# Gate columns of an mLSTM branch taken from a value projection instead of from products of their own

## The chip, the cores and the metric

The kernel runs on one core of one Trainium2 chip. The metric is the device time of one execution in microseconds. The chip was run on the kernel before three times: 1974.41, 1974.73 and 1976.49 us, median 1974.73 us.

## What is computed

The reference is a two-layer backbone over 512 latent tokens and 256 context tokens of width 1024, all in float32. Each layer normalises and modulates its input (h), projects it once, runs three mixers side by side (A: differential attention, B: a bidirectional chunkwise mLSTM, C: neighbourhood attention), gates each, merges them and adds the result. The change concerns the 16 gate columns of mixer B, `bg`: two directions, input and forget gate, four heads.

```
aq, ak, av, az, bq, bk, bv, bo, bz, bg, cq, ck, cv, cz, gm = split_proj(h @ w_in)
...
gates = g.reshape(B, T, 2, 2, ML_HEADS).astype(jnp.float32) + gate_b.astype(jnp.float32)
log_i = gates[:, :, :, 0]
log_f = jax.nn.log_sigmoid(gates[:, :, :, 1])
```

From `log_i` and `log_f` mixer B forms running sums and running maxima along the tokens, forwards and backwards, and from these the weights of its attention-like products. Mixer C's values, `cv`, are 512 other columns of the same projection.

## The kernel before

The activations h lie transposed, eight tiles of 128 channels by 768 tokens (512 latent, then 256 context), each as a pair: the value rounded to the matmul's type and the remainder. A weight is split into such a pair too. A product of both is three matmuls (`P3`, line 32). Weights arrive in halves of a unit, 128 x 512 numbers, in the ring `wr`; ScalarE (ACT) casts the rounded part into the ring `wh`, and GpSimd (POOL) or VectorE (DVE) forms the remainder (`Stream.step`, `Stream.lower`). `wh` has four buffers.

Each layer goes through mixer C, mixer A, mixer B, the merge and the output projection. A projection with channels on the partitions (`proj`: keys `ck`, queries `cq`, gates `cz`) takes weights as the stationary operand and 512 latent or 256 context tokens as the moving one. A value projection (`proj_v`: `cv`, `av`, `bv`) takes 128 tokens of h as the stationary operand and 256 weight columns as the moving one. It makes six token tiles of 24 matmuls, each into one buffer of the PSUM ring `pj`, which has two. The code behind a tile (`fin`) copies it out on ACT and DVE and then releases the buffer.

The gate columns are made while the first value projection of mixer C (`cv`, 0) runs. Its caller hands it a function, `hook`. Called ahead of token tile 4 and once more behind tile 5, it is `gate_mm`: 16 matmuls over the 512 latent tokens, then 16 over the 256 context tokens, with 32 stationary columns (the 16 gate weights and their remainders, `wg`). The result, 32 rows by 768 tokens, is copied to a tile `t`. Four matmuls in full float32 with a matrix of ones and zeros (`zsrc`) spread it over 112 rows, one for each direction, head and chunk of 64 tokens, once for the forget gate and once for the input gate. What follows in `fin` of `branch_b_gates` is a chain on [112, 768] rows, mostly on DVE: log-sigmoid, two running sums, a running maximum, reordering, two stores, twelve transposes and 24 small copies into `bcol`. Mixer B waits for its end much later.

The order of the instructions on each engine is made while the program is built. `Sched` keeps a clock for each engine, from a table of costs, and lists of unfinished work (urgent, calm and other chains). Whenever the main line, which issues the projections in a fixed order, reaches a slot, chains that are due by these clocks issue their next step. So a change of a few instructions moves the places at which others are put. On the chip each engine runs its instructions in the order so made.

## Time and profile before

| | us |
|---|---|
| median of three runs | 1974.73 |
| lowest and highest | 1974.41, 1976.49 |
| the profiled execution | 1975.63 |
| its span, first to last instruction | 1973.9 |
| TensorE (PE) busy | 1865.8 |
| VectorE (DVE) busy | 1363.2 |
| ScalarE (ACT) busy | 862.1 |
| GpSimd (POOL) busy | 617.3 |

The profile is one execution. Its views are: a page with busy times; a timeline, in which instructions of a kind are merged, with the start, the length, the operation, what it writes and reads, the count, and the idle time of the engine ahead of it with what ended that; and windows, which give each engine's busy time, the granted clock of TensorE as a share of 2.4 GHz, and the transfers. A name such as `pj<-h,wh` means that `pj` is written from `h` and `wh`. All of a helper's instructions carry the helper's line, so the names tell them apart. Lengths of matmuls overlap; how far apart they are is read from their starts.

### The profile page before, as it was taken

The page shows a single profiled execution, that of the slowest core. Times are in us where ns is not written, and L with a number is a line of the kernel's source. Part 1 is how long each engine was busy: PE and PEld are TensorE (multiplying, and loading weights), DVE is VectorE, ACT ScalarE, POOL GpSimd, SP SyncE. Part 2 cuts the span into 40 slices and gives each one's busy share as a digit, 9 for nine tenths or more (in the row PEclk, how much of TensorE's full clock was granted, in tenths as well). Part 3 has the DMA queues.
Part 4 walks back from the last instruction along what each step waited for, and adds up shares of the span by engine and source line. Part 5 has one row for each costly group of instructions (what it writes and reads, how often), then busy time and mean ns, then how long its engine had stood idle before and what let it go on. Part 6 is the DMA issues. An engine that isn't in the chain of part 4 may idle for free.

```text
span 1973.9 us, 31993 instructions
## 1 busy us (share of the span) xinstructions
PE 1865.8 (95%) x11420; PEld 1636.1 (83%) x11420; DVE 1363.2 (69%) x3165; ACT 862.1 (44%) x1972; POOL 617.3 (31%) x498
## 2 busy tenths in 40 slices
PE   5989999999999999999999898999999999999997
PEld 2879998988889888888887777898979787888886
DVE  6587775888787877687835768676887777743336
ACT  4345544555544553222223444555555444433343
POOL 1242322121222222333334533424222323334454
PEclk9989999999999999999999999999999999999998
DMA  8233323222211122566645423333231212335554
GB/s 316 72 96 102 96 79 97 61 82 65 68 51 51 44 83 76 182 227 200 214 152 169 147 78 111 119 94 109 69 105 54 65 50 69 97 109 186 168 167 124
DMA packets 137247, 222.26 MB, mean 113 GB/s; under 512 B 15984, under 2 KB 47776, under 8 KB 137088
## 3 DMA queue, kind: packets, MB, share of 16 engines
q1 hardware_dynamic: 137088, 220.22, 35.6%
q8 instruction: 91, 1.49, 0.3%
q14 instruction: 68, 0.56, 0.1%
HBM read 177.36 MB, written 28.11 MB: 104 GB/s over the span
## 4 chain that ended last, share of the span: by engine, by line
PE 47%; issue 21%; DVE 17%; POOL 9%; ACT 3%; DMA 2%; SPq 0%; POOLq 0%; DVEq 0%; ACTq 0%
PE pj L379 34%; POOL wh L344 8%; PE gp L379 7%; PE gp L383 3%; DVE p L344 3%; PE sc L379 3%; DVE qk L344 2%; DVE pt L344 2%; DVE t L344 1%; DMA cb<-in_wmodr_dram 1%; DVE v L344 1%; DVE sc L344 1%; ACT wh L344 1%; DVE h L344 1%; ACT p L344 1%
## 5 line engine op out<-in xcount | busy, mean ns | idle before, releaser
L379 PE MATMUL pj<-h,wh 128*128 128x512 f32 (+1 forms) x5664 | 1124.4, 351 | 20.1 <-DVE gz L344 9.9
L379 PEld LDWEIGHTS pj<-h,wh 128*128 128x128 f32 x5664 | 897.3, 191 | 144.0 <-DVE gz L344 10.3
L344 POOL TENSOR_TENSOR wh<-wr,wh 128x512 fp32r<-128x512 f32 x409 | 558.9, 1372 | 1269.4 <-ACT wh L344 1250.8
L344 ACT CAST wh<-wr 128x512 fp32r<-128x512 f32 x416 | 256.9, 620 | 395.5 <-PE pj L379 193.4
L379 PE MATMUL pj<-wh,h 128*128 128x256 f32 x1728 | 239.3, 289 | 4.1 <-DVE h L344 2.5
L379 PEld LDWEIGHTS pj<-wh,h 128*128 128x128 f32 x1728 | 219.7, 193 | 7.1 <-DVE h L344 3.7
L344 DVE TENSOR_TENSOR pt<-gp,pt 128x512 fp32r<-128x512 f32 (+1 forms) x224 | 123.6, 572 | 80.2 <-ACT pt L344 79.2
L344 ACT CAST pt<-gp 128x512 fp32r<-128x512 f32 (+1 forms) x224 | 105.1, 497 | 155.6 <-PE gp L383 155.1
L379 PE MATMUL pj<-v,wh 128*128 128x512 f32 (+1 forms) x576 | 161.6, 357 | 6.5 <-DVE t L344 6.2
L383 PE MATMUL gp<-ident,p 128*128 128x128 f32 x720 | 110.3, 278 | 23.4 <-DVE p L344 15.5
L379 PEld LDWEIGHTS pj<-v,wh 128*128 128x128 f32 x576 | 103.5, 189 | 23.9 <-DVE t L344 7.9
L379 PE MATMUL gp<-pt,v 128*128 128x256 f32 x864 | 120.2, 287 | 0.0
L383 PEld LDWEIGHTS gp<-ident,p 128*128 128x128 f32 x720 | 84.0, 142 | 40.4 <-issue 18.1
L379 PEld LDWEIGHTS gp<-pt,v 128*128 128x128 f32 x864 | 113.0, 195 | 2.0
L344 ACT ACTIVATE t<-pj 128x512 f32<-128x512 f32 (+1 forms) x118 | 63.4, 538 | 99.7 <-PE pj L379 93.5
L379 PE MATMUL pj<-qk,wh 128*128 128x512 f32 (+1 forms) x288 | 102.2, 355 | 0.0
L344 DVE TENSOR_REDUCE mna<-sc 128x1 f32<-128x768 f32 (+1 forms) x80 | 67.8, 847 | 38.5 <-PE sc L379 38.3
L344 DVE SCALAR_TENSOR_TENSOR t<-t,pj 128x512 f32<-128x512 f32 x66 | 38.8, 594 | 73.2 <-PE pj L379 71.2
L344 ACT ACTIVATE p<-sc,mna 128x768 f32<-128x768 f32 (+1 forms) x80 | 65.5, 819 | 53.7 <-DVE mna L344 53.5
L379 PE MATMUL sc<-qk 128*128 128x512 f32 (+1 forms) x360 | 82.0, 336 | 5.0 <-ACT p L344 4.9
L344 DVE CUSTOM_DVE_ANT_0 sc<-cb,prm 128x512 f32<-128x512 f32 x56 | 60.0, 1072 | 25.4 <-DMA cb<-in_wmodr_dram 24.1
L344 DVE TENSOR_TENSOR qk<-t,qk 64x768 fp32r<-64x768 f32 (+1 forms) x64 | 64.0, 1000 | 14.2 <-ACT qk L344 11.8
(157 smaller groups left out, 2208.8 us busy)
## 6 DMA issues: line engine op xcount, KB each, us to landing
wr<-in_wu_dram SPq DMA_DIRECT2D x304, 256.0 KB, 2.9
cb<-in_wmodr_dram SPq DMA_DIRECT2D x64, 256.0 KB, 3.4
wr<-in_wout_dram SPq DMA_DIRECT2D x64, 256.0 KB, 2.8
wr<-in_wbr_dram SPq DMA_DIRECT2D x48, 256.0 KB, 2.9
q<-qk SPq DMA_DIRECT2D x160, 64.0 KB, 2.4
cb<-vd SPq DMA_DIRECT2D x32, 256.0 KB, 3.2
qk<-in_xT_dram SPq DMA_DIRECT2D x16, 384.0 KB, 5.0
pd<-t SPq DMA_DIRECT2D x16, 384.0 KB, 3.9
```

Of the source, the lines that this page charges most:

```text
L344: return f(*args, **kw)
L379: PE.matmul(o, l, r, start=start, stop=stop)
L383: PE.transpose(o, i, idn)
```

## The change

The 16 gate columns are appended to the weights of the first value projection of mixer C, which then has 272 columns (a new input `wcv`, the value and gate columns side by side). Each token tile gets its gate columns as columns 256 to 271 of its PSUM buffer. `fin` of `proj_v` then calls the hook, which is now `spread`: two copies on DVE write the tile's gate columns, repeated twelve times over the chunks, to one of two tiles `t`, six blocks of 112 columns with tokens on the partitions. When all six tiles are spread, twelve transposes bring them to 112 rows by tokens, where the four selecting products stood before. The gate weights `wg`, their load, cast and remainder, `gate_mm` and the selection matrix go. The rings `wr` and `wh` get buffers for 544 columns in place of 512. The two tiles `t` are held from the first token tile to the last transpose.

```
@@ _units
+            cols = base + np.arange(256)
+            u.append((key + (hf,), np.concatenate([cols, BG + np.arange(16)]) if key == ("cv", 0) else cols, hf))
@@ setup
-            SY.dma_start(out=rv, in_=a["wbg"][l])
-            V.tensor_copy(wg[l][:, :, 0:16], rv)
-            V.tensor_tensor(wg[l][:, :, 16:32], rv, wg[l][:, :, 0:16].bitcast(F32), ALU.subtract)
@@ Stream.step
+                n = int(stream[i].shape[-1]) // 2
+                t = ring("wr", [2 * wide])[:, :n]
+                SY.dma_start(out=t, in_=stream[i][:, n * hf:n * hf + n])
...
+                w = ring("wh", [2, 2 * wide], F32R)[:, :, :int(src.shape[-1])]
@@ proj_v
+            nw = wide if hook else 256
-                if j == 4 and hook:
-                    S_.until(lambda: ready.n == DEPTH)
-                    hook(0)
...
+                        mm(ps[:, :nw], h[k][:, hb, 128 * j:128 * j + 128], w[:, wa, c0:c0 + nw],
...
+                    if hook:
+                        yield from hook(j, ps[:, 256:wide])
                     rel("pj")
...
-            if hook:
-                hook(1)
@@ branch_b_gates
-            def gate_mm(s):
...
-                        mm(ps[:32, :n], wg[l][:, k, :], h[k][:, b, o:o + n], k == 0 and b == 0, k == 7 and b == 1)
...
+            def spread(j, src):
+                if j == 0:
+                    for i in range(2):
+                        yield from acq("t")
+                        gx[i] = ring("t", [T])
+                        pad = gx[i][:, 0:6 * R].rearrange("p (j x) -> p j x", x=R)[:, :, 48:64]
+                        GP.memset(pad, 0.0)
+                while gx[j // 3] is None:
+                    yield
+                for gi in range(2):
+                    o0 = R * (2 * (j % 3) + gi)
+                    to = gx[j // 3][:, o0:o0 + R]
+                    to = bass.AP(to.tensor, to.offset, [list(to.ap[0]), [64, 2], [12, 4], [1, 12]])
+                    V.tensor_copy(to, src.rearrange("p (d g h) -> p d g h", d=2, g=2)[:, :, gi]
+                                  .unsqueeze(3).to_broadcast([128, 2, 4, 12]))
+                hit(gflag)
...
-                yield from wait(gflag, 2, "P")
+                yield from wait(ready, DEPTH)
+                yield from wait(gflag, NT, "P")
...
-                        mm(p[:R, :n], zsrc[0:32, 48 + R * gi:48 + R * gi + R], gr[0][:32, o:o + n], True, True)
+                        for b in range(n // 128):
+                            j = o // 128 + b
+                            o0 = R * (2 * (j % 3) + gi)
+                            tr(p[:R, 128 * b:128 * b + 128], gx[j // 3][:, o0:o0 + R], ident)
...
-                rel("t")
+                rel("t"), rel("t")
```

The change moves instructions that it doesn't name, since the scheduler's clocks differ. The order differs from the first value projection of layer 0 to the first part of mixer A there, and in layer 1 from the first value projection to the first part of mixer A; elsewhere it is the same. Three places follow, before and after.

TensorE in layer 0, from the first value projection (`pj<-wh,h`) to the first keys (`pj<-h,wh`), before:

```order
L379 MATMUL pj<-wh,h 128x256 x96
L379 MATMUL pj<-h,wg_173 32x512 x16
L379 MATMUL pj<-wh,h 128x256 x48
L379 MATMUL pj<-h,wg_173 32x256 x16
L379 MATMUL pj<-h,wh 128x512 x3
L379 MATMUL gp<-t,zsrc 112x512
L379 MATMUL pj<-h,wh 128x512 x9
L379 MATMUL gp<-t,zsrc 112x256
L379 MATMUL pj<-h,wh 128x512 x6
L379 MATMUL gp<-t,zsrc 112x512
```

and after:

```order
L381 MATMUL pj<-wh,h 128x272 x144
L381 MATMUL pj<-h,wh 128x512 x12
L385 MATMUL gp<-ident,t 112x128 x4
L381 MATMUL pj<-h,wh 128x512 x9
L385 MATMUL gp<-ident,t 112x128 x2
L381 MATMUL pj<-h,wh 128x512 x3
L381 MATMUL pj<-h,wh 128x256 x6
L385 MATMUL gp<-ident,t 112x128 x4
L381 MATMUL pj<-h,wh 128x256 x18
L385 MATMUL gp<-ident,t 112x128 x2
```

The gate products are gone, and the transposes (`gp<-ident,t`) stand in four groups, the first behind twelve key products.

VectorE in layer 0, in the chain of the gates: `v` and `pt` of 112 rows are the chain (the scans are listed as `SCALAR_TENSOR_TENSOR pt<-pt,t` and `v<-v,pt`), `gz<-gz,pj` empties a PSUM buffer of the gate projection `cz`, `qk<-t,qk` belongs to mixer C's keys and queries. Before:

```order
L344 TENSOR_TENSOR v<-v 112x768 x2
L344 SCALAR_TENSOR_TENSOR pt<-pt,v 112x768
L344 SCALAR_TENSOR_TENSOR pt<-pt,t 112x768
L344 TENSOR_TENSOR qk<-t,qk 64x768 x2
L344 SCALAR_TENSOR_TENSOR pt<-pt,t 112x768
L344 TENSOR_TENSOR v<-pt 112x768
L344 TENSOR_TENSOR v<-v,pt 112x767
L344 SCALAR_TENSOR_TENSOR gz<-gz,pj 128x512
L344 SCALAR_TENSOR_TENSOR v<-v,pt 112x768
L344 TENSOR_TENSOR wh<-wr,wh 128x512
L344 TENSOR_TENSOR v<-pt,v 112x768
L344 SCALAR_TENSOR_TENSOR gz<-gz,pj 128x256
```

and after:

```order
L345 TENSOR_TENSOR v<-v 112x768 x2
L345 TENSOR_TENSOR qk<-t,qk 64x768
L345 SCALAR_TENSOR_TENSOR pt<-pt,v 112x768
L345 TENSOR_TENSOR qk<-t,qk 64x768
L345 SCALAR_TENSOR_TENSOR pt<-pt,t 112x768 x2
L345 SCALAR_TENSOR_TENSOR gz<-gz,pj 128x512
L345 TENSOR_TENSOR v<-pt 112x768
L345 TENSOR_TENSOR wh<-wr,wh 128x512
L345 TENSOR_TENSOR v<-v,pt 112x767
L345 SCALAR_TENSOR_TENSOR gz<-gz,pj 128x256
```

The first `gz<-gz,pj` stood behind `v<-pt` and `v<-v,pt` and now stands ahead of both. In layer 1 it stood behind both scans and `v<-pt` and now stands between the two scans.

VectorE in layer 1, where the context part of h (`qk<-qk,gsc,gp` and `h<-qk,modc,h` of 256 tokens) is made during the first value projection, whose tiles leave by `v<-pj,v`. Before:

```order
L344 TENSOR_TENSOR v<-pj,v 128x2x128
L344 SCALAR_TENSOR_TENSOR qk<-qk,gsc_186,gp 128x256 x5
L344 SCALAR_TENSOR_TENSOR h<-qk,modc_184,h 128x256 x3
L344 TENSOR_TENSOR v<-pj,v 128x2x128
L344 SCALAR_TENSOR_TENSOR h<-qk,modc_184,h 128x256 x2
L344 SCALAR_TENSOR_TENSOR qk<-qk,gsc_186,gp 128x256 x3
L344 SCALAR_TENSOR_TENSOR h<-qk,modc_184,h 128x256
L344 COPY t<-pj 32x512
L344 SCALAR_TENSOR_TENSOR h<-qk,modc_184,h 128x256 x2
L344 TENSOR_TENSOR v<-pj,v 128x2x128
```

and after:

```order
L345 TENSOR_TENSOR v<-pj,v 128x2x128
L345 COPY t<-pj 128x2x48 x2
L345 SCALAR_TENSOR_TENSOR qk<-qk,gsc_184,gp 128x256 x5
L345 SCALAR_TENSOR_TENSOR h<-qk,modc_182,h 128x256 x3
L345 TENSOR_TENSOR v<-pj,v 128x2x128
L345 COPY t<-pj 128x2x48 x2
L345 SCALAR_TENSOR_TENSOR h<-qk,modc_182,h 128x256 x2
L345 SCALAR_TENSOR_TENSOR qk<-qk,gsc_184,gp 128x256 x3
L345 SCALAR_TENSOR_TENSOR h<-qk,modc_182,h 128x256 x3
L345 TENSOR_TENSOR v<-pj,v 128x2x128
L345 COPY t<-pj 128x2x48 x2
```

Two copies (`t<-pj`, 2 x 48) stand behind each token tile, two pairs of them within this part of h; the copy of 512 gate columns is gone.

## Rows read from the trace of the kernel before

**Rows 1.** The page, part 1: busy us, share of the span, instructions.

```profile
PE 1865.8 (95%) x11420; PEld 1636.1 (83%) x11420; DVE 1363.2 (69%) x3165; ACT 862.1 (44%) x1972; POOL 617.3 (31%) x498
```

**Rows 2.** Timeline, layer 0, PE: start, us, operation, count, idle before.

```profile
47.86 9.14 PE L379 MATMUL pj<-wh,h 128*128 128x256 f32 x74 [0.98 <-DVE h L344]
...
56.84 3.86 PE L379 MATMUL pj<-h,wg 128*32 128x512 f32 x16
...
60.54 5.68 PE L379 MATMUL pj<-wh,h 128*128 128x256 f32 x46
...
66.29 2.04 PE L379 MATMUL pj<-h,wg 128*32 128x256 f32 x16
68.65 0.93 PE L379 MATMUL pj<-h,wh 128*128 128x512 f32 x3 [0.32 <-DVE v L344]
69.51 1.11 PE L379 MATMUL gp<-t,zsrc 32*112 32x512 f32 x2
70.55 2.37 PE L379 MATMUL pj<-h,wh 128*128 128x512 f32 x9
72.84 0.68 PE L379 MATMUL gp<-t,zsrc 32*112 32x256 f32 x2
73.45 1.66 PE L379 MATMUL pj<-h,wh 128*128 128x512 f32 x6
```

**Rows 3.** Timeline, layer 1, first value projection: PE and VectorE (DVE).

```profile
1141.80 3.86 PE L379 MATMUL pj<-h,wg 128*32 128x512 f32 x16
...
1145.50 5.92 PE L379 MATMUL pj<-wh,h 128*128 128x256 f32 x48
1145.70 0.68 DVE L344 COPY t<-pj 32x512 f32<-32x512 f32 x1
1146.31 0.86 DVE L344 SCALAR_TENSOR_TENSOR h<-qk,modc,h 128x256 fp32r<-128x256 f32 x2
```

**Rows 4.** Timeline, layer 0 behind the gate columns: PE, then DVE.

```profile
102.97 4.90 PE L379 MATMUL pj<-h,wh 128*128 128x512 f32 x12 [4.87 <-DVE gz L344]
...
128.35 0.64 PE L383 MATMUL gp<-ident,pt 112*128 112x112 f32 x2 [3.09 <-DVE pt L344]
...
99.05 1.84 DVE L344 TENSOR_TENSOR v<-pt 112x768 f32<-112x768 f32 x1
100.92 1.28 DVE L344 TENSOR_TENSOR v<-v,pt 112x767 f32<-112x767 f32 x1
```

**Rows 5.** Timeline, layer 1 behind the gate columns: PE, then DVE.

```profile
1188.55 1.65 PE L379 MATMUL pj<-h,wh 128*128 128x256 f32 x6 [3.52 <-DVE gz L344]
...
1182.37 4.15 DVE L344 TENSOR_TENSOR_SCAN pt<-pt,t 112x768 f32<-112x768 f32 x2
1186.56 1.22 DVE L344 TENSOR_TENSOR v<-pt 112x768 f32<-112x768 f32 x1
```

**Rows 6.** Windows: busy us (count) of PE, PEld, DVE, ACT, POOL; clock, DMA, GB/s.

```profile
102.00:122.00 20.00, 19.03 (x98) 16.23 (x99) 18.60 (x34) 7.32 (x19) 8.89 (x7) 0.87 0.42 129
...
128.00:148.00 20.00, 18.88 (x112) 16.86 (x113) 14.53 (x56) 8.11 (x22) 4.60 (x5) 0.84 0.28 75
...
1186.00:1196.00 10.00, 7.45 (x42) 7.24 (x43) 9.44 (x10) 2.16 (x4) 3.86 (x4) 0.68 0.29 91
```

**Rows 7.** Timeline, layer 1, PE: four transposes and the products behind them.

```profile
1206.85 0.63 PE L383 MATMUL gp<-ident,p 128*128 128x128 f32 x4 [2.23 <-DVE p L344]
1207.23 3.67 PE L379 MATMUL pj<-h,wh 128*128 128x512 f32 x15
```

**Rows 8.** Timeline, layer 0: GpSimd's split of weights, VectorE's copy of gate columns.

```profile
65.08 4.23 POOL L344 TENSOR_TENSOR wh<-wr,wh 128x512 fp32r<-128x512 f32 x3 [21.55 <-ACT wh L344]
...
68.42 0.40 DVE L344 COPY t<-pj 32x256 f32<-32x256 f32 x1
```

**Rows 9.** Timeline, layer 0, DVE: cast of the gate weights, next h.

```profile
42.30 1.30 DVE L344 CAST wg<-t 128x128 fp32r<-128x128 f32 x1
...
44.02 1.40 DVE L344 SCALAR_TENSOR_TENSOR h<-qk,modc,h 128x512 fp32r<-128x512 f32 x2
```

More of the change, by code (lines that the diff above doesn't have):

```diff
@@ L53, in addv @@
         for hf in range(2):
-            u.append((key + (hf,), base + np.arange(256), hf))
+            cols = base + np.arange(256)
+            u.append((key + (hf,), np.concatenate([cols, BG + np.arange(16)]) if key == ("cv", 0) else cols, hf))
     for g in range(2):
@@ L351 @@
     PE = nc.tensor
+    wide = 272
     bufs = dict(wr=5, wh=4, qk=2, q2=3, v=2, pt=2, p=5, t=4, gz=2, o=3, cb=6, h=KD,
@@ L439 @@
     V.tensor_scalar(cf, cf, 0.5, None, ALU.mult)
-    wg = [const.tile([128, KD, 32], F32R, name=f"wg{l}") for l in range(DEPTH)]
     gb = [const.tile([R, 2], F32, name=f"gb{l}") for l in range(DEPTH)]
     bcol = const.tile([128, NT, 2, 2, 4], F32, name="bcol")
-    zsrc = const.tile([R, 48 + 2 * R], F32, name="zsrc")
+    zsrc = const.tile([R, 48], F32, name="zsrc")
     msk = const.tile([128, 3, 256], BF16, name="mskc")
@@ L511, in srcs @@
     def srcs(l, key):
+        if key == ("cv", 0):
+            return [a["wcv"][l, hf] for hf in range(2)]
         if key[0] in ("cv", "av", "bv"):
@@ L541, in step @@
                     break
-                t = ring("wr", [512])
-                SY.dma_start(out=t, in_=stream[i][:, 512 * hf:512 * hf + 512])
+                n = int(stream[i].shape[-1]) // 2
+                t = ring("wr", [2 * wide])[:, :n]
+                SY.dma_start(out=t, in_=stream[i][:, n * hf:n * hf + n])
                 self.raws[self.loaded] = (t, S_.cur.settle())
@@ L554, in step @@
                     break
-                w = ring("wh", [2, 512], F32R)
+                w = ring("wh", [2, 2 * wide], F32R)[:, :, :int(src.shape[-1])]
                 ACT.copy(out=w[:, 0], in_=src)
@@ L1349, in branch_b_gates @@
         def branch_b_gates():
-            gr, gflag = [None], Flag()
-            def gate_mm(s):
-                o, n = segs[s]
-                S_.need("pj")
-                ps = ring("pj", [512])
-                for k in range(KD):
-                    need(hfl[k][s])
-                    for b in range(2):
-                        mm(ps[:32, :n], wg[l][:, k, :], h[k][:, b, o:o + n], k == 0 and b == 0, k == 7 and b == 1)
-                    if k % 2:
-                        S_.slot()
-                def ev():
-                    yield from first(s, gr, "t")
-                    V.tensor_copy(gr[0][:32, o:o + n], ps[:32, :n])
-                    rel("pj")
-                    hit(gflag)
-                S_.urgent(ev())
+            gx, gflag = [None, None], Flag()
+            def spread(j, src):
[14 more added lines that the diff above has]
+                hit(gflag)
             def fin():
@@ L1470, in branch_b_gates @@
             S_.urgent(fin())
-            return gate_mm
+            return spread
         def b_head(hd, qk, vt, vflag, gz, zflag):
@@ L1847, in _b_consts @@
 def _b_consts():
[L1848 removed]
+    sel = np.zeros((R, 48), np.float32)
     mask = np.zeros((R, 2, T), np.float32)
@@ L1861, in _b_consts @@
                 mask[r, 1] = (pos >= 64 * scan) & (pos < 64 * scan + 64)
-                for gi in range(2):
-                    for part in range(2):
-                        sel[16 * part + 8 * d + 4 * gi + hd, 48 + R * gi + r] = 1.0
     return sel, mask
@@ L1896, in _layout @@
             else:
-                wu[l, u] = w[4 * hf:4 * hf + 4][:, :, cols].transpose(1, 0, 2).reshape(128, 1024)
+                part = w[4 * hf:4 * hf + 4][:, :, cols].transpose(1, 0, 2).reshape(128, -1)
+                if key[:2] == ("cv", 0):
+                    wcv[l, hf] = part
+                wu[l, u] = part[:, :1024]
     o["wu"] = wu
-    o["wbg"] = f["w_in"][:, :, BG:BG + 16].reshape(DEPTH, KD, 128, 16).transpose(0, 2, 1, 3)
+    o["wcv"] = wcv
     o["wbr"] = f["w_br"].reshape(DEPTH, 3, 4, 128, 4, 256).transpose(0, 1, 4, 3, 2, 5).reshape(DEPTH, 3, 4, 128, 1024)
```

6 lines of the change are left out of this document (2 added, 4 removed).

## The prediction

> **What bounds the kernel now.** I read the page first: TensorE (PE) is busy for 95% of the span [rows 1]. So a product that leaves PE's queue is time, unless PE then waits there for somebody else. The next view is therefore the timeline of PE, and in it the marks of idle time. Two kinds of place matter. The first is the stretch in which the gate columns are made, once in each layer: PE runs without a gap through value products, gate products and the first key products [rows 2, 3]. The second comes ten to thirty microseconds later, where the vector work that the gate columns start (the scans of the forget gates) has filled VectorE's queue. There PE stands idle for 4.87 us and 3.09 us in layer 0 and for 3.52 us in layer 1 [rows 4, 5], and it runs at the lower of its two levels (1.2 GHz) for a while afterwards. The granted clock of 0.87 over 20 us means 5.2 us at half speed, 0.84 over 20 us means 6.4 us, and 0.68 over 10 us means 6.4 us, and in these windows VectorE is busy for 18.60 of 20, 14.53 of 20 and 9.44 of 10 us [rows 6]. So the change touches a stretch that PE bounds and, behind it, one that VectorE bounds, and the two have to be priced apart. I count against the profiled execution, 1975.63 us, which is 0.90 us above the median of the three times (1974.73).
>
> **Gate products, removed.** In layer 0 the 16 products of 512 columns start at 56.84 and the next value product at 60.54: 3.70 us. The 16 of 256 columns go from 66.29 to 68.33 (68.65 less the idle 0.32): 2.04 us. The 0.32 us is a wait for a PSUM buffer of the ring pj, which the second gate product had taken [rows 2]. Without that product the first key product uses the buffer of token tile 4, which is free by then. So 3.70 + 2.04 + 0.32 = 6.06 us leave PE's queue. Layer 1 has the same: 1145.50 less 1141.80 is 3.70 again [rows 3]; for the rest I take 2.36 from layer 0.
>
> **Wide value products, added.** 144 products a layer get 272 columns where they had 256. Products of 256 columns follow each other every 0.121 us (74 in 8.98 us, from 47.86 to 56.84), and those of 512 columns every 0.231 us (16 in 3.70 us) [rows 2]. That is 0.43 ns a column, so 16 columns are 6.9 ns, and 144 of them 1.0 us a layer. The ends are 0, if the spacing of 0.121 us were set by the load of the stationary operand alone, and 15.8 us a layer if 272 columns cost as much as 512; I take the slope, because both rows are streams with one load to a product.
>
> **Selecting products out, transposes in.** The four products through the selection matrix take 1.04 and 0.61 us (69.51 to 70.55, 72.84 to 73.45) [rows 2], and the second pair repeats that: 3.30 us a layer. In their place stand 12 transposes. Four of the same kind take 0.38 us in the trace (1206.85 to 1207.23) [rows 7], so 12 cost 1.14 us and 2.16 us are won. The upper end is double, 2.28 us, for the lower clock. They wait for the last spread on VectorE, with twelve key products (2.8 us) ahead of them in PE's queue. The Trainium skill (TensorE: Matmul & The Clock Gate, Part 4: PE-mode transpose) gives about 275 ns for one transpose in a kernel. By that 24 would take 6.6 us, as much as the products they replace, and the sum below would be 4.3 us smaller. The 0.38 us for four speaks against it, being a spacing where the page has a duration [rows 7].
>
> **The spread, and what stands behind it.** Each token tile gets two copies of 96 elements out of PSUM before its pj buffer is released. The nearest row is the copy of 256 elements a partition, 0.40 us [rows 8]; I take 0.2 us each, between 0.1 and 0.4. pj has two buffers, PE needs 2.9 us to fill one, and releasing it 0.4 us later is hidden. Twelve copies are 2.4 us of VectorE a layer; the two copies that go were 0.68 and 0.40 us [rows 3, 8]. In layer 0 VectorE has room in this stretch. In layer 1 it has none, as the next part shows. The padding memsets on GpSimd, the 32 extra columns of each split and the lost small loads cost or give nothing that PE sees. The first key weights are another matter: they can be split only while token tile 5 frees their buffers, and GpSimd needs 1.4 us for one (4.23 us for three) [rows 8]. Before, the second gate product covered that. Now key products could start some 0.1 us late (between 0 and 1.4).
>
> **A cover that goes in layer 1.** The first gate product stood between token tile 3 and token tile 4, and tiles 4 and 5 need the context columns of h, which VectorE is still making. Its last piece ends at 1147.17 (1146.31 + 0.86); token tile 4 starts at 1145.50 and wants the eighth piece 2.5 us later, at 1148.0 [rows 3]. Without the gate product PE is there at 1142.5 and wants the eighth piece at 1145.0. The piece itself comes about 0.4 us later than before, since eight spread copies (1.6 us) enter ahead of it, one copy (0.68 us) goes and the queue absorbs some. PE then waits 2.4 us or somewhat more in place of 3.70 us of products. I take 2.4; the ends are 1.5 and 3.7. Layer 0 has no such wait: its h is ready early.
>
> **The opening.** In layer 0 a cast of the gate weights (1.30 us) stands ahead of h on VectorE [rows 9], and PE idles 0.98 us for h before 47.86 [rows 2]. The cast goes; I take 1.0 us, between 0 and 1.3.
>
> **Sum on PE's queue.** Layer 0: 6.06 - 1.0 + 2.16 - 0.1 = 7.1. Layer 1: the same less 2.4 = 4.7. With the opening 1.0: 12.8 us.
>
> **The stalls behind it.** The order of VectorE changes too. In layer 0 the evacuation of gz, for which PE waits 4.87 us, now stands ahead of two steps of the gate chain, 1.84 and 1.28 us [rows 4]; the chain starts about as much earlier as PE does, so some 3.1 us of that wait go. In layer 1 it stands ahead of one scan (half of 4.15) and a subtraction (1.22): 3.3 of 3.52 us [rows 5]. If the gaps shrink that far, the lower level of the clock should not follow. It costs half of the time that PE works in it: from 102.97 to 107.2 that is 2.1 us, from 1188.55 to 1192.4 it is 1.9 us [rows 4 to 6]. Together 3.1 + 2.1 + 3.3 + 1.9 = 10.4 us. But VectorE's queue is not shorter, and what is late next is its first row minimum of the scores, for which ScalarE's exponentials and through them PSUM buffers wait. I give back a quarter, 2.5 us, and keep 7.9. The 3.09 us wait of layer 0 with the 3.0 us of low clock behind it belongs to the transposes of the finished columns; they move behind more products, and I count nothing for it, since it can reappear at the next buffer. The forecast is 12.8 + 7.9 = 20.7 us: 1975.6 - 20.7 = 1954.9, and 1954.0 against the median.
>
> **Rivals.**
> - *VectorE holds the second stretch.* The stalls and the low clock move but stay as long, because VectorE has as much to do there as before [rows 6]. Then only 12.8 us are won: 1961.9 against the median. For it: 18.60 busy of 20 us, and 9.44 of 10. Against it: the gate chain is urgent for nobody at that moment, and the new order puts PE's need ahead of it.
> - *All of the stalls go.* Then 2.5 us are not given back, and the 3.09 us and the 3.0 us behind it go as well: 20.7 + 8.6 = 29.3, so 1945.4. For it: the transposes that waited 3.09 us now stand behind 24 products more. Against it: something else is late next.
> - *A wide product is dear.* If the spacing of a product of 272 columns were that of one of 512, 0.231 us, 288 products would cost 31.7 us where I count 2.0, and the kernel would be about 9 us slower: 1984. It decides from 0.200 us a product on, where 0.072 us more over 288 products eat the forecast's 20.7 us. Nothing in the trace has such a step between 256 and 512 columns, but no row lies in between.
> - *Nothing to measure.* The context piece in layer 1 could come later than I count, with a lower clock after the wait, and the stalls behind could grow by what PE won: within 4 us of before.
> - *The change does not do what it says.* The order shows the 64 gate products gone and the 288 wide ones in place, so I give that no chance.
>
> **How the numbers follow.** Forecast 0.50, VectorE holds 0.29, all stalls go 0.14, dear wide products 0.04, nothing to measure 0.03. The forecast's own range, with half or all of the 10.4 us, is 1951 to 1957. The range that should hold 8 times in 10 reaches to both gain rivals: 1945 at the lower end, and 1963 at the upper, which is the first rival with 1 us more lost in layer 1. About 0.2%, 4 us, is what a measurement here can tell from no change. Faster by more than that: 0.93, same 0.03, slower 0.04.
>
> **What would show it.** Right: no gate product; token tiles of the first value projection 3.05 us apart; 12 transposes in four groups of 0.2 to 0.4 us; a gap on PE of about 2.4 us ahead of token tile 4 in layer 1, released by VectorE's h; the waits for gz under 2 us and the clock at its upper level after them. Wrong: token tiles of over 3.5 us (dear products); key products starting more than 1 us late for the weights' split; waits for gz as long as before or replaced by waits for a row minimum of the same length, which would give the first rival.

## The result and the profile after

The changed kernel takes 1953.56 us (median of four runs, 1950.75 to 1954.62) against 1974.57 us of the kernel before on the same chip. The ratio is 0.9891, with a 95% interval of 0.9874 to 0.9908: 1.1% faster, 21 us. The profiled execution of the changed kernel took 1954.28 us, with a span of 1952.5. The page's first line answers to [rows 1]:

```profile
PE 1853.1 (95%) x11364; PEld 1627.7 (83%) x11364; DVE 1357.6 (70%) x3180; ACT 864.5 (44%) x1972; POOL 621.4 (32%) x503
```

TensorE (PE) does 12.7 us less, VectorE (DVE) 5.6 us less, and PE is still busy for 95%. 56 products fewer are listed: 64 gate products and 8 selecting products go, 24 transposes come; the remaining 8 I put down to records that the trace lacks. The next fence is PE's timeline in layer 0 from the first value projection to the last transpose of gate columns, against [rows 2] (start, us, operation, count, idle before):

```profile
46.99 15.55 PE L381 MATMUL pj<-wh,h 128*128 128x272 f32 x122 [0.96 <-DVE h L345]
62.38 2.94 PE L381 MATMUL pj<-h,wh 128*128 128x512 f32 x12
65.16 0.60 PE L385 MATMUL gp<-ident,t 128*112 128x128 f32 x4
65.51 2.33 PE L381 MATMUL pj<-h,wh 128*128 128x512 f32 x9
67.68 0.38 PE L385 MATMUL gp<-ident,t 128*112 128x128 f32 x2
67.81 1.65 PE L381 MATMUL pj<-h,wh 128*128 128x512 f32 x9
```

From the same product on, the first key product comes 15.39 us later (62.38 less 46.99); before, it came 20.79 us later (68.65 less 47.86). There is no gap ahead of it. Four transposes delay the next product by 0.35 us, two by 0.13.

Behind it, in the stretch that VectorE bounded, PE's idle marks in layer 0 answer to [rows 4]:

```profile
90.51 3.04 PE L381 MATMUL pj<-h,wh 128*128 128x512 f32 x12 [1.42 <-DVE gz L345]
100.81 0.51 PE L381 MATMUL gp<-qk 128*128 128x256 f32 x2 [1.13 <-ACT p L345]
108.05 0.63 PE L385 MATMUL gp<-ident,p 128*128 128x128 f32 x4 [1.60 <-DVE p L345]
```

The wait for gz is 1.42 us where 4.87 stood, and no wait of 3.09 us follows. The windows there (columns as in [rows 6]) show the clock at its upper level, 2.4 GHz, where [rows 6] had 0.87 and 0.84, with VectorE busy for 18.73 and 18.60 us of 20 where [rows 6] had 18.60 and 14.53:

```profile
90.00:110.00 20.00, 16.76 (x94) 14.07 (x94) 18.73 (x31) 7.22 (x19) 13.94 (x11) 1.00 0.39 123
115.00:135.00 20.00, 18.42 (x130) 16.45 (x129) 18.60 (x65) 9.30 (x25) 5.60 (x6) 1.00 0.35 100
```

Layer 1 is another picture. First the value projection, against [rows 3], then PE's idle marks behind the gate columns, against [rows 5]:

```profile
1122.38 2.72 PE L381 MATMUL pj<-wh,h 128*128 128x272 f32 x19
1125.27 1.43 PE L381 MATMUL pj<-wh,h 128*128 128x272 f32 x9 [0.16 <-DVE h L345]
...
1133.25 2.02 PE L381 MATMUL pj<-h,wh 128*128 128x512 f32 x8
...
1161.73 0.97 PE L381 MATMUL pj<-h,wh 128*128 128x256 f32 x6 [1.18 <-DVE gz L345]
1174.38 0.80 PE L381 MATMUL gp<-qk 128*128 128x256 f32 x2 [5.31 <-ACT p L345]
1185.83 0.63 PE L385 MATMUL gp<-ident,p 128*128 128x128 f32 x4 [1.70 <-DVE p L345]
1192.13 2.03 PE L381 MATMUL gp<-pt,cb 128*128 128x256 f32 x6 [3.79 <-DVE pt L345]
```

The context part of h is late, as forecast: 66 products from 1122.38 to 1133.25 take 10.87 us where 66 times 0.126 make 8.3, so 2.5 us are lost. They are lost in four short waits from token tile 4 on and not in one gap; the four idle marks sum to 1.23 us only, since the lengths of matmuls overlap. The wait for gz has shrunk from 3.52 to 1.18 us, but the waits behind it have grown. For `p` PE waits 5.31 us where the kernel before waits 2.22, in this row:

```profile
1199.78 0.51 PE L379 MATMUL gp<-qk 128*128 128x256 f32 x2 [2.22 <-ACT p L344]
```

For `pt` it waits 3.79 us where the longest such wait in that stretch was 0.54. The wait ahead of the transposes of `p` is shorter, 1.70 us where [rows 7] has 2.23, and one of 1.58 us for `q` at 1184.56 us of the trace before is gone. ScalarE's `p` waits for VectorE's first row minimum, `m`; ScalarE's (ACT) row, VectorE's timeline and GpSimd's (POOL) show what stands ahead of that:

```profile
1173.76 0.47 ACT L345 ACTIVATE p<-gp,m 128x256 f32<-128x256 f32 x1 [7.26 <-DVE m L345]
...
1161.59 2.02 DVE L345 TENSOR_TENSOR_SCAN pt<-pt,t 112x768 f32<-112x768 f32 x1
1163.65 1.23 DVE L345 TENSOR_TENSOR v<-pt 112x768 f32<-112x768 f32 x1
1164.91 1.93 DVE L345 TENSOR_TENSOR v<-v,pt 112x767 f32<-112x767 f32 x1
1166.88 2.09 DVE L345 TENSOR_TENSOR_SCAN v<-v,pt 112x768 f32<-112x768 f32 x1
1169.00 1.22 DVE L345 TENSOR_TENSOR v<-pt,v 112x768 f32<-112x768 f32 x1
1170.15 1.61 DVE L345 CAST v<-v 112x768 fp32r<-112x768 f32 x1
1171.79 0.96 DVE L345 TENSOR_TENSOR v<-v 112x768 fp32r<-112x768 f32 x1
1172.67 0.42 DVE L345 TENSOR_REDUCE m<-gp 128x1 f32<-128x256 f32 x1
...
1158.21 5.87 POOL L345 TENSOR_TENSOR cb<-mskc,t 128x256 f32<-128x256 bf16 x4 [1.89 <-DMA t<-in_rpb_dram]
```

Seven steps of the gate chain run without a break from 1161.59 to 1172.67, 11.1 us; the row minimum comes behind them.

**Where the 21 us came from.** I call lead the start of a product in the trace before, less the start of the same product after. In the first value projection of layer 0 (47.86 against 46.99) it is 0.87 us, of which 0.71 stand at the first product of all (13.88 against 13.17). Over all the runs below, of either way of making the gate columns, that first product starts anywhere from 13.17 to 14.32 us, so the 0.71 us can't be put down to the change. At the last key products ahead of the gz wait (85.38 against 76.27) it is 9.11, so PE's queue won 8.2. When the order is the same again, in mixer A (312.69 against 292.85), it is 19.8: the second stretch of layer 0 won 10.7 us. In layer 1 the lead is 18.5 at 1132.52 and 23.2 at 1170.34, so the queue won 4.7; behind the stalls, at 1391.18, it is 20.8, so the second stretch lost 2.4. Windows over each second stretch agree; the first pair is the kernel before, the second the changed one:

```profile
80.00:280.00 200.00, 187.32 (x1260) 172.60 (x1260) 152.30 (x378) 103.40 (x267) 62.32 (x59) 0.95 0.33 97
1140.00:1240.00 100.00, 88.63 (x542) 75.11 (x541) 79.16 (x164) 45.32 (x102) 35.11 (x29) 0.97 0.32 96
```

```profile
80.00:280.00 200.00, 192.37 (x1352) 177.54 (x1351) 154.15 (x403) 105.77 (x280) 65.69 (x61) 0.99 0.34 100
1140.00:1240.00 100.00, 86.83 (x549) 78.10 (x549) 81.37 (x173) 49.57 (x115) 39.53 (x33) 0.93 0.35 100
```

In layer 0 PE's busy time in 200 us rises by 5.05 us and the clock from 0.95 to 0.99, which is 8 us of full clock. In layer 1 both fall.

**Where layer 0's 10.7 us lie.** Between these points the order differs, so there I read the lead by the work that PE has done: the columns of its products, summed in both traces, an estimate good to about 1 us. By the times of the kernel before it is 9.0 us at 96, 16.0 at 156, 13.5 at 252 and 20.3 at 276. So the stalls of [rows 4] gave about 7 us. Some 2.5 us went again where the changed kernel waits 1.91 us for gz at 160.06 us, with the clock at 0.89 over 155 to 170 us. And nearly 7 us came from a third stall, which none of the rows so far shows: at 258 to 262 us the kernel before waits 0.98, 0.21 and 1.72 us for `p` in mixer C, and the clock is low behind it. The last of these waits and the window around it:

```profile
261.60 1.09 PE L383 MATMUL gp<-ident,p 128*128 128x128 f32 x4 [1.72 <-DVE p L344]
...
255.00:275.00 20.00, 17.09 (x120) 16.43 (x119) 15.63 (x51) 10.82 (x35) 5.02 (x6) 0.83 0.36 116
```

The changed kernel has no wait in that place:

```profile
236.00:256.00 20.00, 20.00 (x169) 19.77 (x168) 15.04 (x49) 11.02 (x34) 6.14 (x8) 1.00 0.46 139
```

The gate chain's transposes end 125 us earlier, at about 133 us. But the third stall goes with the order of layer 0: of the runs below, the three that keep the old order there (layer 1 alone, wide products alone, products away) have it, with a wait of 1.72 or 1.73 us, and the five others that have the changed kernel's order there (layer 0 alone, products back, both cuts of the chain, GpSimd's sums cleared) have no wait above 0.3 us in that place.

### The profile page after: what moved, and what is told of

Same layout as the page of the kernel before. It is cut to its first block, busy times and chain, and to the rows that moved or that the text cites. A ratio compares the mean times of both kernels' runs of the same rounds, so it can differ in the third digit from the quotient of the medians.

```text
span 1952.5 us, 31891 instructions
## 1 busy us (share of the span) xinstructions
PE 1853.1 (95%) x11364; PEld 1627.7 (83%) x11364; DVE 1357.6 (70%) x3180; ACT 864.5 (44%) x1972; POOL 621.4 (32%) x503
## 3 DMA queue, kind: packets, MB, share of 16 engines
q8 instruction: 90, 1.47, 0.3%
## 4 chain that ended last, share of the span: by engine, by line
PE 38%; issue 28%; DVE 14%; POOL 13%; DMA 5%; ACT 2%; POOLq 0%; SPq 0%; DVEq 0%; ACTq 0%
PE pj L381 28%; POOL wh L345 11%; PE gp L381 5%; PE sc L381 3%; PE gp L385 3%; DVE p L345 3%; DMA cb<-in_wmodr_dram 2%; DVE sc L345 2%; DVE qk L345 2%; POOL cb L345 2%; DVE t L345 1%; DVE pt L345 1%; DVE v L345 1%; DVE h L345 1%; DMA v<-in_wmod_dram 1%
## 5 line engine op out<-in xcount | busy, mean ns | idle before, releaser
L345 POOL TENSOR_TENSOR wh<-wr,wh 128x512 fp32r<-128x512 f32 (+1 forms) x410 | 558.6, 1368 | 1237.1 <-ACT wh L345 1209.7
L345 ACT CAST wh<-wr 128x512 fp32r<-128x512 f32 (+1 forms) x416 | 257.4, 621 | 386.7 <-PE pj L381 192.1
L381 PE MATMUL pj<-wh,h 128*128 128x256 f32 (+1 forms) x1728 | 240.2, 289 | 4.7 <-DVE h L345 2.9
L385 PE MATMUL gp<-ident,p 128*128 128x128 f32 x720 | 110.7, 278 | 20.9 <-DVE p L345 15.1
L345 POOL TENSOR_TENSOR cb<-mskc,t 128x256 f32<-128x256 bf16 x64 | 53.1, 864 | 61.4 <-PE gp L381 38.5
```

Source lines behind the costliest of these rows:

```text
L345: return f(*args, **kw)
L381: PE.matmul(o, l, r, start=start, stop=stop)
L385: PE.transpose(o, i, idn)
```

## Experiments

All ratios are to the kernel before on the same chip, with 95% intervals; 0.001 is 2 us. The medians of the kernel before lay between 1974.3 and 1978.1 us over the chips, so ratios are compared, not medians. Three theories stood at this point. *Order:* the stalls of layer 0 went because VectorE's steps stand in another order. *Products:* they went because PE has less to do. *VectorE holds:* what is left is VectorE's gate chain, which cannot be ordered away.

**One layer at a time.** The choice between the two ways of making the gate columns was made for each layer; the order of the layer with the change is that of the changed kernel, the other that of the kernel before.

```
+NEW = (True, False)          # and (False, True)
-            nw = wide if hook else 256
+            nw = wide if hook and NEW[l] else 256
...
+                if j == 4 and hook and not NEW[l]:
+                    S_.until(lambda: ready.n == DEPTH)
+                    hook(0)
...
```

Both kernels also hold three kinds of small tiles (`ms`, `rr`, `rt`) in two buffers in place of six, which is no part of the question. In layer 0 of the first, PE keeps its distance to the changed kernel to 0.1 us from 74 to 675 us, so nothing of it is seen there.

Layer 0 alone: 

> The change in layer 0 alone; layer 1 makes its gate columns as before. The order of the instructions is that of the changed kernel in layer 0 and that of before in layer 1. By the trace of the changed kernel nearly the whole gain lies in layer 0 (PE is 20.2 us ahead at the wait near 466 us, 0.7 of it from the start): then about 19 us faster than before, 1955.5 us. As the prediction split it (opening 1.0, queue 7.1, stalls 5.2 less 1.2) layer 0 brings 12 us: 1962.5.

Layer 1 alone: 

> The change in layer 1 alone; layer 0 as before. By the trace of the changed kernel layer 1 brings 2 us, since new waits of 5.31 and 3.79 us and the low clock behind them take what the products gave: 1972.5 us. As the prediction split it (queue 4.7, stalls 5.2 less 1.2) it brings 8.7 us: 1966.

Layer 0 alone gave 0.9920 (0.9905 to 0.9935), 1960.48 us. Layer 1 alone gave 1.0008 (0.9995 to 1.0021), 1977.24 us: nothing. Layer 0 is between what the trace (1955.5) and the prediction's split (1962.5) made of it, and layer 1 gains less than either. The trace of layer 1 alone has the same new waits, with the releasers of the changed kernel:

```profile
1195.37 0.79 PE L385 MATMUL gp<-qk 128*128 128x256 f32 x2 [5.29 <-ACT p L348]
...
1213.07 2.04 PE L385 MATMUL gp<-pt,cb 128*128 128x256 f32 x6 [3.78 <-DVE pt L348]
```

So they belong to layer 1's own order and are not made by what layer 0 won. Both runs fall short by several microseconds that the two stretches don't show; the last section says where a part of them may be.

**Wide products alone.** In the kernel before, with its order, 120 of the 144 first value products a layer were given 272 columns (the extra 16 are neighbouring weights and are not used).

```
-                        mm(ps[:, :256], h[k][:, hb, 128 * j:128 * j + 128], w[:, wa, c0:c0 + 256], ...)
+                        l_, r_, nw = h[k][:, hb, 128 * j:128 * j + 128], w.rearrange("p a n -> p (a n)"), 256
+                        S_.run("P", 109.0, [l_, w[:, wa, c0:c0 + 256]], [ps[:, :256]])
+                        if hook and not (wa and c0):
+                            nw = 272
+                        PE.matmul(ps[:, :nw], l_, r_[:, 512 * wa + c0:512 * wa + c0 + nw], ...)
```

> The kernel before, in its own order, with 272 columns in 120 of the 144 products of the first value projection of each layer; the 16 extra columns hold nothing that is used. Slope of the prediction: 240 x 6.9 ns = 1.7 us more than before, 1976.3 us, and token tiles of 3.04 us in place of 2.90. If the extra columns were free: 1974.6. If a product of 272 columns cost as much as one of 512: 240 x 0.110 = 26 us more, 2001.

Measured 1.0001 (0.9987 to 1.0016), 1974.43 us. Dear wide products (2001 us) are excluded. The 1.7 us and nothing at all cannot be told apart by the times; in the timeline the spacing is 0.126 us, 5 ns above 256 columns.

**Products away, order kept.** The kernel before with 60 of its 64 gate products left out on the chip, while the scheduler still counts them; the gate values are then not those of the reference.

```
-                        mm(ps[:32, :n], wg[l][:, k, :], ...)
+                        if k or b:
+                            S_.run("P", max(107.0, 0.4167 * n) + 2.0, ...)
+                        else:
+                            mm(ps[:32, :n], wg[l][:, k, :], ...)
```

> The kernel before with the order of all its instructions, from which only 60 of the 64 gate products are left out on the chip (so the gate values are wrong). If the stalls go because the order is another, they stay here: the queue gives 5.4 us in layer 0 and 5.4 less 2.4 for the context piece of h in layer 1, 8.4 us together: 1966.2 us, and the waits for gz stay near 4.9 and 3.5 us. If the stalls go because the chain of the gates starts earlier, they shrink here too: about 1957 us.

Measured 0.9996 (0.9982 to 1.0009), 1973.10 us. The order theory had expected 1966; even that was too much. PE's timeline in layer 0:

```profile
65.78 0.93 PE L379 MATMUL pj<-h,wh 128*128 128x512 f32 x3 [2.05 <-DVE v L344]
...
100.09 4.42 PE L379 MATMUL pj<-h,wh 128*128 128x512 f32 x12 [4.86 <-DVE gz L344]
...
125.46 0.41 PE L383 MATMUL gp<-ident,pt 112*128 112x112 f32 x2 [3.09 <-DVE pt L344]
```

About half of the time of the products (2.5 of some 5.4 us are won up to the first key product) turns into waits for a buffer of pj that VectorE (v) has yet to empty (0.69 us at 57.59 and the 2.05 us above), and the waits of [rows 4] stand there within 0.01 us. In the old order, products leaving PE's queue do not shorten the stalls behind.

**Order kept, products back.** The other corner: the changed kernel in its own order, with 64 products as idle work (32 rows of the buffers of token tiles 4 and 5, which the tile's own products overwrite), not counted by the scheduler.

```
+                for k in range(KD if hook and j in (4, 5) else 0):
+                    n = 512 if j == 4 else 256
+                    for b in range(2):
+                        PE.matmul(ps[:32, :n], W.get(m0)[:, 0, 0:32], h[k][:, b, 0:n], ...)
```

> The changed kernel, instruction for instruction in its order, with the 64 gate products put back as idle work (32 rows of the PSUM buffer of token tiles 4 and 5, overwritten by the tile's own products); they are not counted by the scheduler, so nothing else moves. Two by two with the kernel before, the changed kernel and the run that kept the old order without the products. If the waits went because of the order: the waits for gz in layer 0 stay at 1 to 2 us with the clock up, and the time is that of the changed kernel plus 2 x 5.74 us of products less the 2.5 us that they fill in layer 1 (wait for the context part of h): 1953.6 + 9.0 = 1962.6. If the waits went because the products went: waits of 4.9 and 3.1 us come back in layer 0 with their low clock, 1953.6 + 9 + 10 = 1973.

Measured 0.9943 (0.9929 to 0.9957), 1961.68 us, where the order theory said 1962.6 and the other 1973. The products are back and the stalls are not:

```profile
56.85 3.87 PE L850 MATMUL pj<-h,wh 128*32 128x512 f32 x16
...
96.58 3.04 PE L381 MATMUL pj<-h,wh 128*128 128x512 f32 x12 [1.41 <-DVE gz L345]
```

| | products in | products out |
|---|---|---|
| old order | 1 | 0.9996 (0.9982 to 1.0009) |
| new order | 0.9943 (0.9929 to 0.9957) | 0.9891 (0.9874 to 0.9908) |

In the old order the products are worth 1 us, which the interval can't tell from nothing, in the new one 10 us (8 by the medians). The new order is worth 11 us with the products and 21 without. The order theory holds against the products theory. But the row "new order" is the whole change without the removal: besides the order, of PE as well as of VectorE, it has the transposes in place of the selecting products, the wider products and rings and the spread. That VectorE's order did it is read from the place of gz in it, and was not tried apart.

**Is the order a matter of the chain's place?** Two edits to the scheduler, each in both kernels. The first enters the gate chain among the calm work, the second gives a scan the price of the traces.

```
-            S_.urgent(fin())
+            S_.calm(fin())
```

Changed kernel, calm chain: 

> The changed kernel with the gate chain (log-sigmoid, scans, maxima) entered in the scheduler's calm list in place of its urgent one. If the waits that are left (5.31 and 3.79 us in layer 1 with some 5 us of low clock, 1 to 2 us each in layer 0) are those of a chain that stands ahead of PE's needs on VectorE, they shrink by half or more: 1953.6 less 6 to 10, about 1945. If VectorE simply has that much to do in that stretch, whatever stands first, the waits only move: 1951 to 1957. If the gate columns then come too late for mixer B: above 1958, with a wait on PE for bcol or for B's masks.

Kernel before, calm chain: 

> The kernel before with the gate chain in the calm list; products, selection and copies as before. If the place of the chain on VectorE made its stalls (4.87, 3.09, 3.52 us and three low-clock stretches), most of them go without a product being removed: about 1963. If the stalls are VectorE's whole work, nothing: 1972 to 1977.

```
+                if name == "tensor_tensor_scan":
+                    cost = 2.05 / 768 * 1000.0 * n
```

Changed kernel, scan price: 

> The changed kernel, with one price in the scheduler's table set to what the traces show: a scan of 768 columns takes 2.0 to 2.1 us on VectorE, the table has 0.87. Nothing else is edited; the order of the second stretch follows the new clock. If PE waits there because the scheduler takes VectorE to be free 3.5 us (three scans) earlier than it is, and so sends products whose buffers are emptied late, the waits of layer 1 (5.31 and 3.79 us, 5 us of low clock) shrink by about 3.5 us each where the clock was wrong: 1953.6 less 4 to 8, about 1948. If what matters is how much VectorE has to do there: 1951 to 1957. As with the calm list, a new order can also lose elsewhere: above 1960.

Kernel before, scan price: 

> The kernel before with the same one price. Its stalls (4.87, 3.09, 3.52 us, three low-clock stretches) stand behind scans too. If the wrong price made them: 8 to 12 us less, about 1964. If the new order of the stretch was won by the shorter queue of PE and VectorE and not by where the chain stands: 1971 to 1977.

| edit | before | after |
|---|---|---|
| none | 1 | 0.9891 (0.9874 to 0.9908) |
| calm chain | 1.0015 (1.0005 to 1.0025) | 0.9977 (0.9967 to 0.9987) |
| scan at its price | 1.0047 (1.0030 to 1.0064) | 0.9939 (0.9924 to 0.9954) |

Wherever a gain was expected it did not come: each of the four is slower than the kernel it was made from. With the calm chain the wait of 5.31 us in layer 1 is still 4.83, since the chain's scans still stand ahead of the first row minimum (VectorE is at them and their neighbours from 1161.84 to 1172.60 us); what moved is the chain's end, and its last copies, now 30 us later, meet mixer C's next products. The window shows it, against 86.83 and 0.93 of the changed kernel:

```profile
1140.00:1240.00 100.00, 80.36 (x465) 70.34 (x464) 82.85 (x195) 48.49 (x115) 34.14 (x28) 0.90 0.28 84
```

With the scan at its price the changed kernel's longest wait in that stretch is 2.98 us, but between 80 and 1100 us PE falls 8.6 us behind the changed kernel. So a better price in the scheduler did not make a better order here, and the calm list did not take the chain out of the way: what a chain placed behind the row minimum would give was not tried. But under each of the three schedulers the change itself gains: 1.1, 0.4 and 1.1%. So part of the gain is the change, and several tenths of a per cent hang on which order the scheduler happens to make.

**What the chain costs.** The changed kernel in its order, the chain's vector steps between the absolute value and the transposes cut to 16 of 768 columns on the chip.

```
+                args = [v[:, :16] if hasattr(v, "shape") and _elems(v) == n else v for v in args]
...
```

> The changed kernel, same order, with the vector steps of the gate chain between its absolute value and its transposes cut to 16 of 768 columns on the chip (mixer B's gate weights are then not those of the reference); two small loads fill what is not written. It prices what the chain's time on VectorE, about 25 us a layer, costs PE. If the remaining waits in both layers are the chain's: those of 1.42, 1.13, 1.60, 1.91 us in layer 0 and 1.18, 5.31, 1.70, 3.79 us in layer 1 go but for about 2 us each layer, with the two low-clock stretches of layer 1 (about 5 us): 1953.6 - 17 = 1937. If other vector work holds PE there: above 1948.

Measured 0.9863 (0.9846 to 0.9880), 1946.73 us: a smaller gain than expected, and in part for a reason of the experiment. Of three loads a layer that fill the cut tiles, two stand right ahead of another load, on which VectorE waits (first row VectorE, second PE):

```profile
54.12 0.23 DVE L349 CUSTOM_DVE_ANT_0 t<-t 128x64 f32<-128x64 f32 x1 [5.81 <-DMA t<-in_lamqk_dram]
...
55.31 6.91 PE L385 MATMUL pj<-wh,h 128*128 128x272 f32 x33 [5.01 <-DVE gcol L349]
```

The second run fills the tiles with GpSimd instead.

```
-                nc.sync.dma_start(out=rt2[:R, 2:4], in_=a["bmask"])
+                nc.gpsimd.memset(rt2[:R, 2:4], 0.0)
...
```

> The kernel with the gate chain cut to 16 columns on VectorE once more, the tiles now filled by GpSimd in place of two loads on SyncE's queue, which in the first such run put 5.0 us of waiting and a low clock into layer 0 (VectorE waited for a load behind them). Expected without that: 1946.7 less 5 to 8.4, so 1938 to 1942; layer 0 gains 4.5 us on the changed kernel and layer 1 about 14. If the first value stands, 1946, the loads were not its reason.

Measured 0.9807 (0.9786 to 0.9828), 1939.92 us, inside what was expected; by the ratios 0.84% below the changed kernel, 16.6 us. In the second stretches (as above) PE's busy time is 196.52 and 95.40 us with the clock at 1.00 and 0.98:

```profile
80.00:280.00 200.00, 196.52 (x1399) 182.35 (x1398) 145.68 (x408) 110.90 (x289) 60.53 (x62) 1.00 0.34 101
1140.00:1240.00 100.00, 95.40 (x612) 86.22 (x611) 77.80 (x197) 58.04 (x134) 40.59 (x37) 0.98 0.40 114
```

In layer 1 the waits of 1.18, 5.31 and 1.70 us are gone, and one of 3.48 us for `pt` stays in place of 3.79. By the lead on the changed kernel layer 1's stretch wins 12.6 us with the clock (2.5 at 1148.76, 15.1 at 1210.61). In layer 0 the waits of 1.42, 1.13 and 1.60 us are gone, which wins 4.9 us, and the wait of 1.91 us for gz at 160 us stays. So VectorE's time for the chain is what holds PE in layer 1 but for the last wait, and most of what still holds it in layer 0.

**GpSimd beside the chain.** Chain steps of two inputs over 768 columns take 0.96 us in some places and 1.2 to 2.0 in others. The changed kernel in its order, GpSimd's sums `cb<-mskc,t` replaced by clearing the tile (mixer C's mask and table are left out).

```
-                        GP.tensor_tensor(bt[:, e].rearrange(...), msk[:, v].rearrange(...), w0, ALU.subtract)
+                        nc.gpsimd.memset(bt[:, e], 0.0)
```

> The changed kernel, same order on every engine, with GpSimd's sum of mask and position table of mixer C (two inputs, 256 columns) replaced by clearing the tile (mixer C's mask and table are left out). In the traces the chain's vector steps of 768 columns take 0.96 us where GpSimd stands still and 1.2 to 1.9 us beside these sums, and the sums 0.64 us alone and 1.47 us beside the chain. If GpSimd's sums slow VectorE down: the five chain steps beside them fall to about 1 us each, 2 to 3 us a layer; the wait of 5.31 us in layer 1 becomes 2.5 to 3.5, and the time 1953.6 less 3 to 6, about 1949. If the longer steps have another cause: no change, 1952 to 1956.

Measured 0.9870 (0.9849 to 0.9892), 1949.29 us. The interval overlaps that of the changed kernel, so the time leaves it open. The trace does not (VectorE, then GpSimd, then PE, layer 1):

```profile
1158.80 0.96 DVE L345 TENSOR_TENSOR v<-pt 112x768 f32<-112x768 f32 x1
1159.79 0.96 DVE L345 TENSOR_TENSOR v<-v,pt 112x767 f32<-112x767 f32 x1
...
1152.00 1.07 POOL L979 MEMSET cb<- 128x256 f32 x4
...
1168.50 0.80 PE L381 MATMUL gp<-qk 128*128 128x256 f32 x2 [4.02 <-ACT p L345]
```

The steps of 1.23 and 1.93 us are 0.96 each, and the wait of 5.31 is 4.02, less of a change than expected; in layer 0 the waits of 1.13 and 1.60 become one of 1.92. By the lead the two stretches win 1.2 us (0.18 at 80.40, 1.38 at 151.83) and 2.3 us (4.25 at 1148.76, 6.59 at 1198.57). The 4.02 us that are left are not the chain alone. GpSimd's splits of weights (`wh<-wr,wh`) now fall beside its next steps: the last scan takes 2.73 us where 2.09 stood, and `v<-pt,v` 1.87 us where 1.22 stood.

## Why the prediction was right, and where its steps were wrong

The total, 1954.0, was within a microsecond of 1953.56. Some 60% of the gain is PE's queue (8.2 and 4.7 us), which was read correctly. The rest came out near the forecast by luck: behind the queue two errors of 6 to 7 us cancel, one in each layer.

- **Gate products:** 6.06 us forecast. Over 122 wide products, 20.79 less 15.39 is 5.40 us, and adding what these products cost more (122 times 4.8 ns, 0.6 us) gives 6.0. Right.
- **Wide products:** 6.9 ns each, 1.0 us a layer, forecast; 15.39 us for 122 are 126.1 ns where 121.4 stood, 4.8 ns, 0.7 us a layer. Right in kind, and the rival of dear products fell.
- **Selection and transposes:** 12 transposes take 0.35 + 0.13 + 0.35 + 0.14 = 0.97 us (1.14 forecast). An estimate by the Trainium skill's figure for one transpose, of bfloat16 values (TensorE: Matmul & The Clock Gate, Part 4: PE-mode transpose), makes 3.3 us a layer; the trace's spacing of about 0.08 us decides.
- **First key weights:** no wait at 62.38, 0.1 us forecast.
- **The cover in layer 1:** 2.4 us forecast, 2.5 measured, released by h, from the place named on, though in four waits and not in one gap. Right.
- **The queue's sum:** 7.1 and 4.7 us forecast, leads of 8.2 and 4.7 measured.
- **The opening:** 1.0 us forecast for the cast that goes; between the product at 41.32 (now 40.56) and the one at 47.86 (now 46.99) only 0.1 us was won; most of the lead at 46.99 is the earlier first product. The step that failed took the cast's 1.30 us for the cast's own. GpSimd in the kernel before, then VectorE and GpSimd in the changed kernel, against [rows 9]:

```profile
39.14 4.38 POOL L344 TENSOR_TENSOR wh<-wr,wh 128x512 fp32r<-128x512 f32 x3 [36.97 <-ACT wh L344]
```

```profile
41.70 1.37 DVE L345 CUSTOM_DVE_ANT_0 t<-t 128x64 f32<-128x64 f32 x1
...
38.39 4.60 POOL L345 TENSOR_TENSOR wh<-wr,wh 128x544 fp32r<-128x544 f32 x3 [36.22 <-ACT wh L345]
```

  The next instruction of the same kind takes 0.21 us. This one ends at 43.07, just after GpSimd's third split at 42.99; before, the cast ended at 43.60 and GpSimd's third split at 43.52. By these ends the time was a wait for GpSimd, and it passed to the instruction that moved up.
- **The stalls behind, layer 0:** 5.2 us of stall and clock were forecast to go, less a share of the quarter given back (2.5 us), and the wait of 3.09 us with its low clock was counted as nothing. 10.7 us were won. That is the size of the rival *all of the stalls go*, but not its mechanism. The stalls named gave about 7 us: against "I count nothing for it, since it can reappear at the next buffer", the wait of 3.09 us shrank to 0.36 and 0.25 us. Some 2.5 us of that were lost again at 160 us, and the rest came from the stall at 258 us, which no term and no rival of the prediction has.
- **The stalls behind, layer 1:** the same 5.2 us less the same share were forecast, and 2.4 us were lost. The step that failed is the quarter: "what is late next is its first row minimum of the scores" named the right wait, but its price was not a quarter of 10.4 us, it was the whole of layer 1's share and 2.4 us more. This layer went the way of the rival *VectorE holds the second stretch*. The argument for that rival, VectorE's 9.44 us of 10, was the better one here; against it the prediction set an order in which PE's need comes first, and that order has PE's first need ahead of seven chain steps and its second need behind them.
- **What the splits and buffers of 544 columns cost:** "cost or give nothing that PE sees" does not fit the last section, where products are slower in every kernel with the wider buffers; the cause is open.

That the order took the stalls of layer 0, and not the shorter queue, is shown by the two-by-two table. That it was VectorE's order, as the prediction says, fits the wait for gz and is not shown for the stall at 258 us. The prediction did not see that removing the products without a new order would be worth 1 us. Why the scheduler's new order is kind to layer 0 and not to layer 1 was not settled; two edits that should have improved it by its own logic made both kernels slower.

## What to carry to other kernels

Work taken off the busiest engine is worth its time only where that engine doesn't then wait for the next one: here the same 64 products were worth 1 us or nothing in one order and 8 to 10 us in another. When a stretch is bounded by a second engine, price the wait that comes after the one you remove by the whole queue ahead of it, up to its full length, and do so for each place apart. A time that stands on a row can be a wait inside the instruction; look at what the other engines end at that moment before you count it as won. And follow the lead past the stalls that you named: nearly 7 us of what layer 0 won came from a stall 125 us behind the chain.

## What the runs showed of the hardware

**VectorE waits for GpSimd.** A step of two inputs over 768 columns takes 0.96 us alone, 1.2 to 1.4 us beside GpSimd's sums and 1.9 to 2.0 us beside a split of weights; a cast of one input takes 0.55 us alone and 1.61 us beside a split. The sums themselves take 1.47 us each (5.87 for four) where two take 1.28 us when VectorE doesn't work on such steps. GpSimd's clearing of a tile adds nothing: a step beside one split takes 2.00 us in the changed kernel (at 1155.12), and the same step beside one split and four clearings takes 2.01 us in the kernel that clears (at 1150.87). The Trainium skill says this (SBUF — State Buffer, Who interferes with whom): a VectorE instruction with two SBUF inputs contends with a GpSimd instruction that reads SBUF, and not with one that only writes it. The traces agree with both halves, by the steps of two inputs just named.

**Products of 512 columns are slower in the kernels with wider buffers.** In the output projection of layer 1, which the change doesn't touch and where PE waits for nothing and the clock is full, 48 products take longer. First the kernel before, then the changed one, each at one of the projection's units, which are all alike; the start of the row behind gives the spacing:

```profile
1789.32 11.04 PE L379 MATMUL pj<-h,wh 128*128 128x512 f32 x48
1800.20 0.39 PE L379 MATMUL pj<-v,wh 128*128 128x512 f32 x1
```

```profile
1783.73 11.26 PE L381 MATMUL pj<-h,wh 128*128 128x512 f32 x48
1794.82 0.39 PE L381 MATMUL pj<-v,wh 128*128 128x512 f32 x1
```

That is 10.88 against 11.09 us, 227 against 231 ns a product. All nine kernels with rings of 544 columns have the longer spacing, layer 1 alone among them (11.26 us for 48), and all five with 512 the shorter, wide products alone among them (11.04): so it comes with the rings and not with the wide products. Products of 256 columns are not slower: the median spacing of `pj<-h,wh` is 120 ns before and 119 after. Over all back-to-back products less than 300 ns apart, of 256 and 512 columns, the mean spacing of `pj<-h,wh` is 181.5 ns before and 182.4 after, and of `pj<-v,wh` 194.9 and 198.9. For 5664 and 576 products that is some 5 + 2 = 7 us, an estimate from these means, and an upper end, since what falls into waits costs nothing. It fits the lead that the changed kernel loses outside its two stretches (0.5 us in each 26 us of that projection). It also fits the two single-layer kernels: each pays for the wider rings once, the changed kernel once for both layers, so their gains together should fall short by one such cost. Added up they make a ratio of 0.9928 where the changed kernel has 0.9891, 7 us apart, though the intervals would allow 2 to 12. Whether it is the rings' width, where the tiles then lie, or something else that came with them is open. Rings of 512 columns with a place of their own for the two wide units were not tried; no version that was run beats the changed kernel with its whole computation.
